# Row pitch of the activation tiles in a two-layer streaming encoder: 320 columns for the matmul inputs, 288, 304, 320 and 256 for the SwiGLU outputs

## The chip, the cores and the metric

The kernel runs on one NeuronCore of a Trainium2 chip. What counts is device time in microseconds (us) of one execution; three runs of a kernel are timed, and their median is taken. The engines are PE (TensorE, matmul; its weight loads are shown apart as PEld), DVE (VectorE), ACT (ScalarE), POOL (GpSimd) and SP, which issues most DMA transfers.

## The reference

The program is a trunk of two layers over 16 meta tokens and 256 frames, 272 tokens of 1024 features, in float32. Layer 0 mixes tokens by differential attention, layer 1 by a sparse attention with an indexer. Each mixer stands between two half-weighted SwiGLU feed-forwards:

```python
for layer in range(DEPTH):                      # DEPTH = 2
    h = h + 0.5 * _swiglu(_rms_norm(h, ln_ffn1[layer]), ffn1_wi[layer], ffn1_wo[layer])
    hn = _rms_norm(h, ln_mix[layer])
    ...
    h = h + mix @ w_out[layer]
    h = h + 0.5 * _swiglu(_rms_norm(h, ln_ffn2[layer]), ffn2_wi[layer], ffn2_wo[layer])
return h[:, N_META:]

def _swiglu(x, wi, wo):                         # wi: 1024 x 5632, wo: 2816 x 1024
    a, b = jnp.split(x @ wi, 2, axis=-1)
    return (jax.nn.silu(a) * b) @ wo
```

## The kernel before

Features lie on the 128 partitions and tokens along the free dimension: `h` is [128, 8, 272], eight rows of 272 tokens in each partition, one row for each block of 128 features. A float32 product is made of three passes in the type float32r, whose values are split into a high and a low part: `mm3` (lines 245 to 248) issues high weights by high rows (L246), high weights by low rows (L247) and low weights by high rows (L248), into one PSUM tile. Each matmul has its own weight load.

`prep_x` scales a row of `h` and splits it into `xh` and `xl`, the tiles that `X["h"]` and `X["l"]` point to. They are the moving operand of the gate-and-up product of every feed-forward and of the projections of both attentions. A feed-forward (`ffn`) first runs over 22 blocks of hidden features: for each it takes one weight tile, and for each of the eight rows k of xh and xl it issues three matmuls into a gate tile `pa` and three into an up tile `pb`, 48 in all. So each row is read by six matmuls in a run. DVE and ACT then form silu(gate) times up and split it into row j of `ah` and `al` (22 rows each). In its second half `ffn` makes eight output blocks from these: for each it runs over the 22 rows of ah and al, three matmuls a row, 66 matmuls into a tile `pc`. There are four feed-forwards. The first three work on 272 tokens; the last one leaves out the meta tokens and works on 256 (`c0=NM`), and its X tiles lie in the storage of the tile `W`, which before held the relative-position bias.

Before the change every one of these rows is 272 columns from the next. The projections of queries and keys in the first attention read the rows of xh and xl in order for one output tile after the other, so each row is read by three matmuls in a run. In the sparse attention, `cqh` and `cql` are the split latent of the queries, [128, 2, 256], the moving operand of `q_abs`.

Weights come from HBM through SP's queue into `wr` tiles; ACT makes the high part `wh`, DVE the low part `wl`, in rotating buffers of 2048 columns. All tiles are placed by pools, in the order in which the code asks for them. In the built program the tiles begin, in bytes within a partition, at 27136 (xh), 35840 (xl), 46720 (W), 152512 and 176448 (ah and al of the first feed-forward), 148224 and 172160 (ah and al of the others), 177536 and 179584 (cqh and cql); the weight buffers begin at 88704 (wh) and 121472 (wl) and every 8192 bytes after these. A matmul reads 128 weight columns, 512 bytes, at a multiple of 512 bytes within its buffer.

Of the kernel before, what the change touches and what calls it, by code (L numbers as in the profile page):

```python
# [11 lines left out]
F32 = mybir.dt.float32  # L12
F32R = mybir.dt.float32r
BF = mybir.dt.bfloat16
AF = mybir.ActivationFunctionType
OP = mybir.AluOpType
# [5 lines left out]
KT = D // 128  # L22
SEQ = 256
NM = 16
T = NM + SEQ
DFF = 2816
FT = DFF // 128
# [5 lines left out]
BH = 16  # L33
IH = 8
NREL = 399

CH = 2048
WARM = 8
# [23 lines left out]
def trunk(ctx, tc, d, out):  # L62
    nc = tc.nc
    PE, ACT, DVE, POOL = nc.tensor, nc.scalar, nc.vector, nc.gpsimd

    const = ctx.enter_context(tc.tile_pool(name="const", bufs=1))
# [6 lines left out]
    ps = ctx.enter_context(tc.tile_pool(name="ps", bufs=1, space=PSUM))  # L73

    def psa():
        return ps.tile([128, 512], F32, name="pa", bufs=3)

    def psb():
        return ps.tile([128, 512], F32, name="pb", bufs=3)
# [90 lines left out]
    h = const.tile([128, KT, T], F32, name="h")  # L170
# [28 lines left out]
    def ln(i):  # L199
        return lambda k: gn[:, 8 * i + k:8 * i + k + 1]  # L200

    X = dict(h=const.tile([128, KT, T], F32R, name="xh"), l=const.tile([128, KT, T], F32R, name="xl"))
    acc = const.tile([128, T], F32, name="acc")
    R = const.tile([128, T], F32, name="R")

# [3 lines left out]

    def prep_x(k, g, c0=0):  # L210
        c = slice(c0, T)
        xh, xl = X["h"], X["l"]
        ACT.activation(xh[:, k, c], h[:, k, c], AF.Copy, scale=g(k))
        DVE.scalar_tensor_tensor(xl[:, k, c], h[:, k, c], g(k), xh.bitcast(F32)[:, k, c],  # L214
                                 op0=OP.mult, op1=OP.subtract)

    def prep_s(k, c0=0):
# [27 lines left out]
    def mm3(ps, wh, wl, bh, bl, start, stop):  # L245
        PE.matmul(ps, wh, bh, start=start, stop=False)  # L246
        PE.matmul(ps, wh, bl, start=False, stop=False)  # L247
        PE.matmul(ps, wl, bh, start=False, stop=stop)  # L248
# [3 lines left out]
    for k in range(KT):  # L252
        c = slice(256 * k, 256 * k + 256)
# [12 lines left out]
    W = const.tile([128, 16, T], F32, name="W")  # L266
# [22 lines left out]
            prep_x(mt, g, c0)  # L289
            prep_s(mt, c0)  # L290

    def ffn(g_next, c0=0, extra=None, first=0):
        c = slice(c0, T)
        with tc.tile_pool(name="act", bufs=1) as actp, tc.tile_pool(name="ev", bufs=2) as ev:
            ah = actp.tile([128, FT, T], F32R, name="ah")
            al = actp.tile([128, FT, T], F32R, name="al")
            ub = {}

            def act_lo(j):
                DVE.tensor_tensor(al[:, j, c], ub.pop(j)[:, c], ah.bitcast(F32)[:, j, c], OP.subtract)  # L300

            def evac(j, pa, pb):
                t = ev.tile([128, T], F32, name="t")
                s = ev.tile([128, T], F32, name="s")
                b = ev.tile([128, T], F32, name="b")
                DVE.tensor_tensor(t[:, c], pa[:, c], R[:, c], OP.mult)  # L306
                last_silu.append(ACT.activation(s[:, c], t[:, c], AF.Silu))
                DVE.tensor_tensor(b[:, c], pb[:, c], R[:, c], OP.mult)
                ws.ahead()
                if j:  # L310
                    act_lo(j - 1)
                DVE.tensor_tensor(b[:, c], s[:, c], b[:, c], OP.mult)  # L312
                ACT.copy(ah[:, j, c], b[:, c])  # L313
                ub[j] = b

            pairs = {}
            for j in range(FT):
                wh, wl = ws.next()
                pa, pb = psa(), psb()
                for k in range(KT):  # L320
                    for m, ps in ((0, pa), (1, pb)):
                        s = slice((2 * k + m) * 128, (2 * k + m + 1) * 128)
                        mm3(ps[:, c], wh[:, s], wl[:, s], X["h"][:, k, c], X["l"][:, k, c],
                            k == 0, k == KT - 1)
                pairs[j] = pa, pb
                if j == first:
                    rstd(psc(), c0)
                    if extra:
                        extra(psc())
                if j >= first:  # L330
                    for i in sorted(pairs):
                        evac(i, *pairs.pop(i))
            act_lo(FT - 1)

            for mt in range(KT):
                ps = psc()
                for half in range(2):
                    wh, wl = ws.next()
                    for kk in range(11):
                        f = half * 11 + kk  # L340
                        s = slice(kk * 128, kk * 128 + 128)
                        mm3(ps[:, c], wh[:, s], wl[:, s], ah[:, f, c], al[:, f, c], f == 0, f == FT - 1)
                    if half == 0:
                        ws.ahead()
                evac_h(mt, ps, True, g_next, c0)
                ws.ahead()

    def diff_attention():
        with tc.tile_pool(name="da", bufs=2) as da, tc.tile_pool(name="dp", bufs=1) as dp:
# [11 lines left out]
            for i in range(2):  # L361
                p = dp.tile([128, 400], F32, name=f"pta{i}")
# [19 lines left out]
            def proj_qk(i):  # L382
                wh, wl = ws.next()
                ps = (psc(), psc()) if i == 1 else (pj(), pj())
                for m in range(2):
                    for k in range(KT):
                        s = slice((2 * k + m) * 128, (2 * k + m + 1) * 128)
                        mm3(ps[m][:, :T], wh[:, s], wl[:, s], X["h"][:, k, :], X["l"][:, k, :], k == 0, k == KT - 1)
                    if i == 0 and m == 0:
                        rstd(ps1())  # L390
                st[i] = dict(ps=ps)
# [21 lines left out]
            def proj_v(i):  # L413
                wh, wl = ws.next()
                ps = pj()
                for k in range(KT):
                    s = slice(k * 128, k * 128 + 128)
                    mm3(ps[:, :T], wh[:, s], wl[:, s], X["h"][:, k, :], X["l"][:, k, :], k == 0, k == KT - 1)
                v = da.tile([128, T], F32, name="v")
                DVE.tensor_tensor(v, ps[:, :T], R, OP.mult)  # L420
                st[i]["v"] = v
# [162 lines left out]
            n = AH  # L584
# [7 lines left out]
            g = [pj(), pj(), None, None]  # L592
# [23 lines left out]
            for grp in (2, 3):  # L616
                w = ws.next()
                for m in range(2):
                    ps = pj()
# [4 lines left out]
    def dsa():  # L624
        q0 = NM
        Q = slice(q0, T)
        with tc.tile_pool(name="sa", bufs=2) as sa, tc.tile_pool(name="sp", bufs=1) as sp, \
# [77 lines left out]
            for m in range(4):  # L705
                ps = ps1()
                for k in range(2):
                    s = slice((2 * m + k) * 128, (2 * m + k + 1) * 128)
# [202 lines left out]
            n = BH  # L911
            for i in range(n):
# [14 lines left out]
                    soft_fin(i - 1)  # L927
                if i >= 3:
                    av(i - 3)
            x2 = const.tile([128, 16, T], F32R, name="W")  # L930
            X["h"], X["l"] = x2[:, 0:KT, :], x2[:, KT:16, :]

            def wout_part(ps, w, m, k0, k1):
                wh, wl = w
# [6 lines left out]
            g = [psc(), None, None, None]  # L941
# [20 lines left out]
            for grp in (2, 3):  # L962
                w = ws.next()
                for m in range(2):
                    ps = psc()
                    wout_part(ps, w, m, 0, 8)
                    evac_h(2 * grp + m, ps, False, ln(5), q0)
                ws.ahead()

    ffn(ln(1), extra=build_bias, first=1)  # L970
    diff_attention()
    once.close()
    ffn(ln(3))
    ffn(ln(4))
    dsa()
    ffn(None, c0=NM)


def _layout(inp):
# [49 lines left out]
    oh = np.zeros((32, 400), f)  # L1029
    for j in range(NREL):  # L1030
        rel = j - 271
# [22 lines left out]
```

## Time and profile before

| | |
|---|---|
| timed runs | 1083.3 us median of 3 (1083.02 to 1084.7) |
| profiled execution | span of 1079.7 us from first to last instruction; no other total of this execution is listed |
| PE | 1067.9 us busy, 8332 matmuls |
| PEld | 1021.7 us busy |
| DVE, ACT, POOL | 689.6, 542.7, 77.2 us busy |
| transfers | 174.20 MB, 161 GB/s on average |

The span is the time between the first and the last instruction of the profiled execution; the timed runs are other executions, and what the runtime adds before and after is in theirs. Matmuls are pipelined: the next one starts long before the record of the last one ends, so start-to-start spacing tells more than a record's length.

### The profile page before, as it was taken

The page shows a single profiled execution, that of the slowest core. Times are in us where ns is not written, and L with a number is a line of the kernel's source. Part 1 is how long each engine was busy: PE and PEld are TensorE (multiplying, and loading weights), DVE is VectorE, ACT ScalarE, POOL GpSimd, SP SyncE. Part 2 cuts the span into 40 slices and gives each one's busy share as a digit, 9 for nine tenths or more (in the row PEclk, how much of TensorE's full clock was granted, in tenths as well). Part 3 has the DMA queues.
Part 4 walks back from the last instruction along what each step waited for, and adds up shares of the span by engine and source line. Part 5 has one row for each costly group of instructions (what it writes and reads, how often), then busy time and mean ns, then how long its engine had stood idle before and what let it go on. Part 6 is the DMA issues. An engine that isn't in the chain of part 4 may idle for free.

```text
span 1079.7 us, 20010 instructions
## 1 busy us (share of the span) xinstructions
PE 1067.9 (99%) x8332; PEld 1021.7 (95%) x8332; DVE 689.6 (64%) x1191; ACT 542.7 (50%) x876; POOL 77.2 (7%) x111
## 2 busy tenths in 40 slices
PE   8999999999999999999999999999999999999998
PEld 7999999998889999999999999999876799999998
DVE  6567645577777666655576666546898657666542
ACT  6455444356687544444454444535856545444331
POOL 1200000042210000000000000000153100000000
PEclk9999999999999999999999999999999999999999
DMA  8985445533343454445654544455422025554461
GB/s 295 210 233 204 151 154 169 190 134 128 128 153 117 166 187 168 172 129 170 213 204 164 188 161 142 161 172 201 156 91 90 1 101 181 189 195 171 147 200 68
DMA packets 30809, 174.20 MB, mean 161 GB/s; under 512 B 3664, under 2 KB 5216, under 8 KB 16896
## 3 DMA queue, kind: packets, MB, share of 16 engines
q1 hardware_dynamic: 29808, 169.99, 46.0%
q0 software_dynamic: 912, 2.95, 1.5%
q8 instruction: 65, 1.06, 0.4%
q14 instruction: 24, 0.20, 0.1%
HBM read 171.47 MB, written 1.46 MB: 160 GB/s over the span
## 4 chain that ended last, share of the span: by engine, by line
PE 92%; DMA 2%; DVE 2%; ACT 1%; issue 1%; POOL 0%; SPq 0%; DVEq 0%; POOLq 0%; ACTq 0%
PE pa L246 11%; PE pa L247 11%; PE pa L248 11%; PE pc L246 9%; PE pc L247 9%; PE pc L248 9%; PE pb L247 8%; PE pb L246 8%; PE pb L248 8%; DMA wr<-w_ffn_wi 2%; PE pc L858 1%; PE pc L861 1%; DVE wl L133 1%; DMA h<-hT 1%; DVE sel L794 1%
## 5 line engine op out<-in xcount | busy, mean ns | idle before, releaser
L116 ACT CAST wh<-wr 128x2048 fp32r<-128x2048 f32 (+3 forms) x180 | 301.0, 1673 | 347.5 <-PE pb L247 176.0
L133 DVE TENSOR_TENSOR wl<-wr,wh 128x2048 fp32r<-128x2048 f32 (+3 forms) x188 | 368.0, 1958 | 48.6 <-PE pc L248 29.4
L246 PE MATMUL pa<-xh,wh 128*128 128x272 f32 (+1 forms) x736 | 213.0, 290 | 2.4 <-ACT wh L255 2.4
L248 PE MATMUL pa<-xh,wl 128*128 128x272 f32 (+1 forms) x736 | 212.7, 289 | 1.5 <-DVE wl L133 1.5
L247 PE MATMUL pa<-xl,wh 128*128 128x272 f32 (+1 forms) x736 | 213.1, 290 | 0.0
L246 PE MATMUL pc<-ah,wh 128*128 128x272 f32 (+1 forms) x704 | 201.6, 286 | 0.0
L247 PE MATMUL pc<-al,wh 128*128 128x272 f32 (+1 forms) x704 | 201.2, 286 | 0.0
L248 PE MATMUL pc<-ah,wl 128*128 128x272 f32 (+1 forms) x704 | 200.9, 285 | 0.0
L247 PE MATMUL pb<-xl,wh 128*128 128x272 f32 (+1 forms) x544 | 157.4, 289 | 0.0
L248 PE MATMUL pb<-xh,wl 128*128 128x272 f32 (+1 forms) x544 | 156.8, 288 | 0.0
L246 PE MATMUL pb<-xh,wh 128*128 128x272 f32 (+1 forms) x544 | 156.0, 287 | 0.0
L246 PEld LDWEIGHTS pa<-xh,wh 128*128 128x128 f32 x736 | 139.0, 189 | 7.3 <-ACT wh L255 3.7
L248 PEld LDWEIGHTS pa<-xh,wl 128*128 128x128 f32 x736 | 138.6, 188 | 2.0 <-DVE wl L133 1.7
L247 PEld LDWEIGHTS pa<-xl,wh 128*128 128x128 f32 x736 | 138.5, 188 | 0.2
L247 PEld LDWEIGHTS pc<-al,wh 128*128 128x128 f32 x704 | 132.6, 188 | 0.0
L248 PEld LDWEIGHTS pc<-ah,wl 128*128 128x128 f32 x704 | 132.5, 188 | 0.0
L246 PEld LDWEIGHTS pc<-ah,wh 128*128 128x128 f32 x704 | 132.3, 188 | 0.0
L306 DVE TENSOR_TENSOR t<-pa,R 128x272 f32<-128x272 f32 (+1 forms) x88 | 38.4, 436 | 117.0 <-PE pa L248 116.6
L246 PEld LDWEIGHTS pb<-xh,wh 128*128 128x128 f32 x544 | 103.1, 189 | 0.0
L247 PEld LDWEIGHTS pb<-xl,wh 128*128 128x128 f32 x544 | 102.5, 188 | 0.2 <-DVE xl L214 0.2
L248 PEld LDWEIGHTS pb<-xh,wl 128*128 128x128 f32 x544 | 102.4, 188 | 0.0
L313 ACT CAST ah<-b 128x272 fp32r<-128x272 f32 (+1 forms) x88 | 36.6, 416 | 75.1 <-DVE b L312 75.1
(326 smaller groups left out, 1723.9 us busy)
## 6 DMA issues: line engine op xcount, KB each, us to landing
wr<-w_ffn_wi SPq DMA_DIRECT2D x85, 1024.0 KB, 4.8
wr<-w_ffn_wo SPq DMA_DIRECT2D x64, 704.0 KB, 4.1
wr<-w_qk SPq DMA_DIRECT2D x8, 1024.0 KB, 4.7
wr<-w_out SPq DMA_DIRECT2D x8, 1024.0 KB, 4.9
wr<-w_v SPq DMA_DIRECT2D x8, 512.0 KB, 3.3
wr<-w_uqa SPq DMA_DIRECT2D x4, 1024.0 KB, 4.8
W<-fd POOLq DMA_DIRECT2D x8, 272.0 KB, 18.9
wr<-w_ffn_wi SPq DMA_DIRECT2D x7, 256.0 KB, 6.5
```

The lines of the kernel that those rows point to most:

```text
L116: ACT.copy(w[:, c], self.raw[i][:, c])
L133: DVE.tensor_tensor(w[:, c], r[:, c], self.h[i].bitcast(F32)[:, c], OP.subtract)
L246: PE.matmul(ps, wh, bh, start=start, stop=False)
L247: PE.matmul(ps, wh, bl, start=False, stop=False)
L248: PE.matmul(ps, wl, bh, start=False, stop=stop)
L306: DVE.tensor_tensor(t[:, c], pa[:, c], R[:, c], OP.mult)
L313: ACT.copy(ah[:, j, c], b[:, c])
L794: DVE.scalar_tensor_tensor(sel[:, b, kc], r[:, kc], wt[:, b, 2 * i + e:2 * i + e + 1], sel[:, b, kc], op0=OP.mult, op1=OP.add)
L858: PE.matmul(ps[:, B1], qas[i][:, 256 * k + 128:256 * k + 256], ckg[:, k, :], start=k == 0, stop=k == 1)
L861: PE.matmul(ps[:, B0], qas[i][:, 256 * k:256 * k + 128], ckg[:, k, 0:144], start=k == 0, stop=k == 1)
```

## The change

Three things change in the layout, and nothing in what is computed. The tiles xh and xl get rows of 320 columns, of which 272 are used (`XS`). The tiles ah and al get rows of 288, 304, 320 and 256 columns in the four feed-forwards (`AS`), and are filled from column 0 also in the last one. The last feed-forward's X tiles are packed to rows of 256 tokens without the meta tokens, with 64 columns left free between the high and the low tile; `X["o"]` is the offset of the first token there. `ffn` is given its number `i`; the loop variable that had this name is now `n`.

The instructions of every engine are the same as before, in the same order. On DVE, after the first attention, two instructions change what they wait for: the first multiplication of the second feed-forward's `t` no longer waits for POOL, and the first `al` does.

Since xh and xl grow by 1536 bytes each, everything behind them moves on by 3072 bytes. In the built program xh begins at 27136 and xl at 37376, W at 49792 (the packed low tile 8448 bytes behind it), ah and al of the four feed-forwards at 155584 and 180928, 151296 and 178048, 151296 and 179456, 151296 and 173824, cqh and cql at 180608 and 182656, wh at 91776 and wl at 124544.

```diff
+XS = 320
+AS = (288, 304, 320, 256)
...
-    X = dict(h=const.tile([128, KT, T], F32R, name="xh"), l=const.tile([128, KT, T], F32R, name="xl"))
+    X = dict(h=const.tile([128, KT, XS], F32R, name="xh"), l=const.tile([128, KT, XS], F32R, name="xl"), o=0)
...
     def prep_x(k, g, c0=0):
         c = slice(c0, T)
-        xh, xl = X["h"], X["l"]
-        ACT.activation(xh[:, k, c], h[:, k, c], AF.Copy, scale=g(k))
-        DVE.scalar_tensor_tensor(xl[:, k, c], h[:, k, c], g(k), xh.bitcast(F32)[:, k, c],
+        xh, xl, xc = X["h"], X["l"], slice(c0 - X["o"], T - X["o"])
+        ACT.activation(xh[:, k, xc], h[:, k, c], AF.Copy, scale=g(k))
+        DVE.scalar_tensor_tensor(xl[:, k, xc], h[:, k, c], g(k), xh.bitcast(F32)[:, k, xc],
...
-    def ffn(g_next, c0=0, extra=None, first=0):
+    def ffn(i, g_next, c0=0, extra=None, first=0):
         c = slice(c0, T)
+        ac = slice(0, T - c0)
+        xc = slice(c0 - X["o"], T - X["o"])
...
-            ah = actp.tile([128, FT, T], F32R, name="ah")
-            al = actp.tile([128, FT, T], F32R, name="al")
+            ah = actp.tile([128, FT, AS[i]], F32R, name="ah")
+            al = actp.tile([128, FT, AS[i]], F32R, name="al")
...
-                        mm3(ps[:, c], wh[:, s], wl[:, s], X["h"][:, k, c], X["l"][:, k, c],
+                        mm3(ps[:, c], wh[:, s], wl[:, s], X["h"][:, k, xc], X["l"][:, k, xc],
...
-                        mm3(ps[:, c], wh[:, s], wl[:, s], ah[:, f, c], al[:, f, c], f == 0, f == FT - 1)
+                        mm3(ps[:, c], wh[:, s], wl[:, s], ah[:, f, ac], al[:, f, ac], f == 0, f == FT - 1)
...
-            x2 = const.tile([128, 16, T], F32R, name="W")
-            X["h"], X["l"] = x2[:, 0:KT, :], x2[:, KT:16, :]
+            x2 = const.tile([128, 17, SEQ], F32R, name="W").rearrange("p k t -> p (k t)")
+            n2 = KT * SEQ
+            X["h"] = x2[:, 0:n2].rearrange("p (k t) -> p k t", t=SEQ)
+            X["l"] = x2[:, n2 + 64:2 * n2 + 64].rearrange("p (k t) -> p k t", t=SEQ)
+            X["o"] = NM
...
-    ffn(ln(1), extra=build_bias, first=1)
+    ffn(0, ln(1), extra=build_bias, first=1)
...
-    ffn(ln(3))
-    ffn(ln(4))
+    ffn(1, ln(3))
+    ffn(2, ln(4))
     dsa()
-    ffn(None, c0=NM)
+    ffn(3, None, c0=NM)
```

## Rows read from the trace of the kernel before

**Rows 1.** The page: busy time, share of the span and instructions; the chain by engine.
```profile
PE 1067.9 (99%) x8332; PEld 1021.7 (95%) x8332; DVE 689.6 (64%) x1191; ACT 542.7 (50%) x876; POOL 77.2 (7%) x111
...
PE 92%; DMA 2%; DVE 2%; ACT 1%; issue 1%; POOL 0%; SPq 0%; DVEq 0%; POOLq 0%; ACTq 0%
```

**Rows 2.** Windows by stage, PE alone: window, its length, busy time, matmuls, clock.
```profile
core 0: us, PE busy (x), PEclk, DMA share, GB/s
145.00:211.00 66.00, 66.00 (x530) 1.00 0.53 176
359.00:480.00 121.00, 121.00 (x970) 1.00 0.48 166
480.90:546.90 66.00, 66.00 (x531) 1.00 0.56 188
679.20:745.00 65.80, 65.80 (x529) 1.00 0.52 175
896.00:1013.80 117.80, 117.80 (x1009) 1.00 0.51 181
1014.00:1076.00 62.00, 62.00 (x528) 1.00 0.43 144
```

**Rows 3.** One line, the full-precision logits of the sparse attention: min/median/max ns.
```profile
L858 PE MATMUL pc<-ckg,qa x48: 392/393/497, 816.8 to 858.6; 128*128 128x272 f32 x48
```

**Rows 4.** Groups by form, PE, second feed-forward's gate-and-up product (359 to 480 us).
```profile
L247 PE MATMUL pb<-xl,wh 128*128 128x272 f32 x162 | 46.8, 289 | 0.0
L248 PE MATMUL pa<-xh,wl 128*128 128x272 f32 x162 | 46.7, 288 | 0.0
L247 PE MATMUL pa<-xl,wh 128*128 128x272 f32 x161 | 46.7, 290 | 0.0
L248 PE MATMUL pb<-xh,wl 128*128 128x272 f32 x162 | 46.6, 288 | 0.0
L246 PE MATMUL pb<-xh,wh 128*128 128x272 f32 x162 | 46.4, 286 | 0.0
L246 PE MATMUL pa<-xh,wh 128*128 128x272 f32 x161 | 45.8, 284 | 0.0
```

**Rows 5.** The same view for one run of row 0, 372.96 to 373.45 us.
```profile
L247 PE MATMUL pb<-xl,wh 128*128 128x272 f32 x1 | 0.3, 292 | 0.0
L248 PE MATMUL pa<-xh,wl 128*128 128x272 f32 x1 | 0.3, 290 | 0.0
L246 PE MATMUL pa<-xh,wh 128*128 128x272 f32 x1 | 0.3, 288 | 0.0
L247 PE MATMUL pa<-xl,wh 128*128 128x272 f32 x1 | 0.3, 288 | 0.0
L248 PE MATMUL pb<-xh,wl 128*128 128x272 f32 x1 | 0.3, 288 | 0.0
L246 PE MATMUL pb<-xh,wh 128*128 128x272 f32 x1 | 0.3, 285 | 0.0
```

**Rows 6.** One tile, cqh, 770 to 802 us: min/median/max ns.
```profile
L246 PE MATMUL pb<-cqh,wh x58: 278/283/388, 769.7 to 801.2; 128*128 128x256 f32 x58
L248 PEld LDWEIGHTS pb<-cqh,wl x58: 187/192/192, 769.9 to 801.4; 128*128 128x128 f32 x58
L248 PE MATMUL pb<-cqh,wl x58: 278/283/283, 770.0 to 801.5; 128*128 128x256 f32 x58
```

**Rows 7.** One tile, W, 896 to 1013.8 us: the last feed-forward's gate-and-up product.
```profile
L247 PE MATMUL pa<-W,wh x168: 274/280/283, 896.1 to 1013.3; 128*128 128x256 f32 x168
...
L246 PEld LDWEIGHTS pb<-W,wh x168: 187/188/188, 896.2 to 1013.4; 128*128 128x128 f32 x168
L246 PE MATMUL pb<-W,wh x168: 276/279/282, 896.3 to 1013.5; 128*128 128x256 f32 x168
```

**Rows 8.** Timeline, PE, sparse attention's query projection; 29 matmuls between the two.
```profile
791.03 0.28 PE L247 MATMUL pb<-cql,wh 128*128 128x256 f32 x1
...
794.63 0.28 PE L247 MATMUL pb<-cql,wh 128*128 128x256 f32 x1
```

**Rows 9.** Timeline, PE, first attention's projection; 47 matmuls between the two.
```profile
217.59 0.29 PE L246 MATMUL pa<-xh,wh 128*128 128x272 f32 x1
...
223.65 0.29 PE L246 MATMUL pc<-xh,wh 128*128 128x272 f32 x1
```

More of the change, by code (lines that the diff above doesn't have):

```diff
@@ L290, in evac_h @@
             prep_s(mt, c0)
-    def ffn(g_next, c0=0, extra=None, first=0):
+    def ffn(i, g_next, c0=0, extra=None, first=0):
         c = slice(c0, T)
+        ac = slice(0, T - c0)
+        xc = slice(c0 - X["o"], T - X["o"])
         with tc.tile_pool(name="act", bufs=1) as actp, tc.tile_pool(name="ev", bufs=2) as ev:
-            ah = actp.tile([128, FT, T], F32R, name="ah")
-            al = actp.tile([128, FT, T], F32R, name="al")
+            ah = actp.tile([128, FT, AS[i]], F32R, name="ah")
+            al = actp.tile([128, FT, AS[i]], F32R, name="al")
             ub = {}
             def act_lo(j):
-                DVE.tensor_tensor(al[:, j, c], ub.pop(j)[:, c], ah.bitcast(F32)[:, j, c], OP.subtract)
+                DVE.tensor_tensor(al[:, j, ac], ub.pop(j)[:, c], ah.bitcast(F32)[:, j, ac], OP.subtract)
             def evac(j, pa, pb):
@@ L312, in evac @@
                 DVE.tensor_tensor(b[:, c], s[:, c], b[:, c], OP.mult)
-                ACT.copy(ah[:, j, c], b[:, c])
+                ACT.copy(ah[:, j, ac], b[:, c])
                 ub[j] = b
@@ L330, in ffn @@
                 if j >= first:
-                    for i in sorted(pairs):
-                        evac(i, *pairs.pop(i))
+                    for n in sorted(pairs):
+                        evac(n, *pairs.pop(n))
             act_lo(FT - 1)
@@ L387, in proj_qk @@
                         s = slice((2 * k + m) * 128, (2 * k + m + 1) * 128)
-                        mm3(ps[m][:, :T], wh[:, s], wl[:, s], X["h"][:, k, :], X["l"][:, k, :], k == 0, k == KT - 1)
+                        mm3(ps[m][:, :T], wh[:, s], wl[:, s], X["h"][:, k, 0:T], X["l"][:, k, 0:T], k == 0, k == KT - 1)
                     if i == 0 and m == 0:
@@ L417, in proj_v @@
                     s = slice(k * 128, k * 128 + 128)
-                    mm3(ps[:, :T], wh[:, s], wl[:, s], X["h"][:, k, :], X["l"][:, k, :], k == 0, k == KT - 1)
+                    mm3(ps[:, :T], wh[:, s], wl[:, s], X["h"][:, k, 0:T], X["l"][:, k, 0:T], k == 0, k == KT - 1)
                 v = da.tile([128, T], F32, name="v")
```

## The prediction

> **What bounds the kernel now.** I read the page first. PE is busy for 99% of the span, and 92% of the chain that ended last is PE work [rows 1]; the granted clock is 1.00 in every stage that I looked at [rows 2], which is the upper of its two levels (2.4 GHz). The spacing of the matmuls therefore sets the time, so the second view was busy time by stage. In stages without a gap, the length of the window divided by its matmuls is the spacing from one start to the next. A window counts the matmuls that its edges cut as well: a record lasts 0.29 us while the next one starts after 0.12 us, so two are to be taken off [rows 2]. That gives:
>
> - gate-and-up product of the second feed-forward, 272 columns: 121.00 us / 968 = 125.0 ns
> - down products of the first, second and third feed-forward, 272 columns: 66.00 / 528 = 125.0, 66.00 / 529 = 124.8, 65.80 / 527 = 124.9 ns
> - gate-and-up product of the last one, 256 columns: 117.80 / 1007 = 117.0 ns
> - its down product, 256 columns: 62.00 / 526 = 117.9 ns
>
> At 2.4 GHz, 272 columns take 113.3 ns and 256 columns 106.7 ns if one column enters in each cycle. Some 10% is lost, and this loss is what a row's place in memory could change. That the chip can do without it shows in the full-precision matmuls of the attention: a record lasts 393 ns for 272 columns in two passes [rows 3]. A record is longer than the spacing by about 162.5 ns, since its end is modelled: in the gate-and-up product the six places have means from 284 to 290 ns, 287.5 on average [rows 4], where the spacing is 125.0. So 393 ns stands for 230.5 ns, or 115 ns a pass, and this I take as the spacing without a stall.
>
> **What the change does.** No instruction is added or removed and none is moved on any engine; two waits on POOL change places on DVE after the first attention, long after POOL's last work there, which costs nothing. ACT and DVE write as many columns as before, each row in one piece, and no DMA changes. What is left is where rows start. A row of 272 columns is 1088 bytes, four times 256 plus 64, so from one row of the contraction to the next the start moves on by 64 bytes in 256, and four starts take turns. 320 columns are five times 256 bytes: every row of xh and xl now starts at a multiple of 256. All weight buffers lie 128 past a multiple of 256, before and after.
>
> **Does the start matter at all?** In the second feed-forward, the six matmuls of row 0, whose start is a multiple of 256, last 288, 288, 290, 285, 292 and 288 ns [rows 5], 288.5 on average against 287.5 for the stage: 126.0 instead of 125.0 ns. So the start that the change gives to all rows belongs to the slower ones, by 1 ns.
>
> **A stage whose rows all have one start.** The projection of the queries in the sparse attention reads cqh and cql: 256 columns, a pitch of 256, every row 128 past a multiple of 256. Its records have a median of 283 ns and reach no more than 283 in the row for the low weights [rows 6]; those of the last feed-forward's gate-and-up product, as wide but with four starts in turn, have medians of 279 and 280 [rows 7]. Start to start it is 30 matmuls in 794.63 - 791.03 = 3.60 us, 120.0 ns without change [rows 8]: a beat into which the matmuls settle, 3.0 ns slower than with four starts. The weight loads under it also take longer, a median of 192 against 188 ns [rows 6, 7]. Weight load and moving rows seem to get into each other's way, at the same place each time.
>
> **The sum, term by term** (number of matmuls by change of spacing):
>
> 1. Gate-and-up products 1 to 3: 3 x 22 x 48 = 3168 matmuls, 125.0 now. The nearest row for what comes is row 0, 126.0; the far one is the settled beat, which adds 3.0: 128.0. I take 126.5, nearer to row 0, which has the same width and start: +1.5 ns, +4.8 us.
> 2. Projections of both attentions that read xh and xl with 272 columns: 576 + 72 = 648. Here each row is read by three matmuls in a run, not six; 48 spacings take 223.65 - 217.59 = 6.06 us, 126.2 ns [rows 9]. To 126.5: +0.2 us.
> 3. Down product of the third feed-forward, pitch 320, every row of ah and al on a multiple of 256: 528 x (126.5 - 124.9) = +0.8 us.
> 4. Down product of the first, pitch 288, two starts in turn (192 and 64 past a multiple): neither is the slow one of row 0, nor is it one start; 0, with 528 x 1 ns = 0.5 us to either side. Down product of the second, pitch 304: the same four starts in the opposite order; 0.
> 5. Gate-and-up product of the last one: 22 x 48 = 1056 matmuls, 256 columns, pitch 256, all rows 128 past a multiple. This is cqh and cql again, in width, pitch, start and order of the weights: 117.0 to 120.0, +3.2 us.
> 6. Its down product, pitch 256, all rows on a multiple of 256: 528 matmuls at 117.9 now, between that and 120.0 then; I take 119.0, +0.6 us.
>
> Sum: 4.8 + 0.2 + 0.8 + 3.2 + 0.6 = +9.6 us on a span of 1079.7, so 1089.3. Between this span and the median of the timed runs, 1083.3, lie 3.6 us, in which nothing changes: 1092.9, about 1093 us, or 0.9% slower. This case's own range has row 0 alone in terms 1 and 3 (126.0: +3.2 +0.6, and term 2 at -0.1), 3.2 for term 5 and 0 for term 6: +6.9, 1090; at the other end 128.0 in terms 1 to 3 (+9.5 +1.2 +1.6) and 120.0 in the last two (+3.2 +1.1): +16.6, 1100.
>
> PE's neighbours stay covered: in the gate-and-up product the page's DVE and ACT work lies below a PE that never pauses, and a slower PE only gives them more room.
>
> **A rule that speaks against it.** Rows show a loss of 10% against one column a cycle [rows 2], and weight loads of 192 ns where moving rows have one start [rows 6]. The Trainium skill says otherwise: its page "SBUF — State Buffer", section "Who interferes with whom", holds that PE never waits for anyone at SBUF, and "TensorE: Matmul & The Clock Gate", section "Step-by-step: what each phase is for", that rows and weights are read through two independent ports, so that a load takes no bandwidth from a running matmul. By these the start of a row would be worth nothing, each term above 0 and the time 1083.3; the trace does not bear it out, since 125.0 ns stands where its own formula, in "Back-to-back issue gap", would give an estimate of 115.8.
>
> **The rivals.**
>
> - *No change.* If the spacing is set by something that merely comes round every four rows, such as the order of the weights, the starts do not matter: terms all 0, 1083 us. Row 0's 1 ns could be this. Against it: the settled 120.0 and the 192 ns loads, in a stage whose weights come in the same order as those of the last feed-forward. It also comes out so if a gain in one stage pays for a loss in another. Chance 0.12.
> - *Faster.* With one start for all rows the matmuls settle into one beat, and which beat depends on the distance between the rows' start and the weights' start. In cqh it is 0 bytes in 256; for xh and xl it is 128 instead, so weight load and moving rows may fall between one another and not on one another. The fastest of the six places now has 284 ns, 121.5 ns of spacing [rows 4]. If all rows of terms 1 to 3 come to that: 3168 x 3.5 + 648 x 4.7 + 528 x 3.4 = 15.9 us; half of it is 8 us; with term 5 unchanged or won as well, 1064 to 1075. The extreme is no stall at all, 115 ns: 4344 matmuls by 10 ns, 43 us, 1040, for which only full-precision passes speak. It decides from the point where term 1 falls below 125.0 - 4800 / 3168 = 123.5 ns, for then the other terms (+4.8 us) are made up. For it: no stage of the trace has 272 columns with one start, so its beat is unknown. Against it: row 0 has the same distance and is slow. Chance 0.30.
> - *Much slower.* The settled beat of xh and xl lies above 128.0: over 1101 us. Single places last up to 292 ns in row 0, that is 129.5. Chance 0.08.
>
> **Chances and range.** The forecast has 0.50, the others 0.12, 0.30 and 0.08. A measurement of this kernel tells a change from none at about 0.2%, 2 us. Slower: 0.50 + 0.08 = 0.58, faster 0.30, the same 0.12. For the range I go up to 1101, which leaves out the much slower 0.08, and down to 1068, which leaves out the better third of the faster case, some 0.10.
>
> **What would show it.** In the changed kernel's profile the spacing by stage is the test. Right: about 126.5 ns in the gate-and-up products 1 to 3, with the six places no longer changing from row to row, 120.0 in the last one with weight loads of 192 ns, and 125 in the down product with pitch 304. Wrong in its mechanism: the last gate-and-up product stays at 117.0, or the four-row pattern lives on with one start. Wrong in sign: the gate-and-up products fall below 123.5. Three feed-forwards with three pitches also tell how much each is worth by itself.

## The result and the profile after

The changed kernel takes 1095.4 us (median of 4 runs, 1090.6 to 1096.5) where the kernel before took 1083.8 beside it (4 runs, 1083.0 to 1084.7): a ratio of the means of 1.0098, 95% interval 1.0072 to 1.0124. The medians are 11.6 us apart and the means 10.6 us, with an interval of 7.8 to 13.4 us. That is about 1% slower; the forecast was 1093. The profiled execution has a span of 1093.3 us (its own time 1095.1), at a mean granted clock of 0.998.

Two lines of the page of the changed kernel: busy time, and the chain that ended last by engine.

```profile
PE 1080.7 (99%) x8332; PEld 1034.5 (95%) x8332; DVE 689.8 (63%) x1191; ACT 542.8 (50%) x876; POOL 77.1 (7%) x111
...
PE 91%; DMA 3%; DVE 2%; ACT 1%; issue 1%; POOL 0%; SPq 0%; DVEq 0%; ACTq 0%; POOLq 0%
```

Against [rows 1] the counts are equal, DVE, ACT and POOL are as busy as before, and only PE (+12.8 us) and its weight loads (+12.8 us) have grown. So the same matmuls come at a longer spacing. The windows by stage of the changed kernel, PE alone, answer to [rows 2]. The columns are window, length, busy time, matmuls, clock, DMA share, GB/s.

```profile
150.20:216.00 65.80, 65.80 (x528) 1.00 0.53 175
400.00:440.00 40.00, 40.00 (x318) 1.00 0.53 182
488.20:554.00 65.80, 65.80 (x527) 1.00 0.56 187
600.00:640.00 40.00, 40.00 (x318) 1.00 0.49 178
688.60:755.00 66.40, 66.40 (x526) 1.00 0.53 173
905.00:1027.00 122.00, 122.00 (x1018) 1.00 0.50 177
1027.20:1089.00 61.80, 61.80 (x523) 1.00 0.43 144
```

Length divided by (matmuls - 2) is the spacing, to 0.1 or 0.2 ns. The lines are the first down product, the second gate-and-up product (40.00 / 316 = 126.6 ns), the second down product (65.80 / 525 = 125.3), the third gate-and-up and the third down product (66.40 / 524 = 126.7), and the last gate-and-up (122.00 / 1016 = 120.1) and last down product (61.80 / 521 = 118.6). From here on a spacing is the mean from start to start of neighbouring matmuls of a stage, from the trace's start times with pauses left out. It agrees with such windows and does not suffer from the few records that a trace lacks:

| stage (matmuls) | before, ns | after, ns | worth, us |
|---|---|---|---|
| gate-and-up 1, 2, 3 (3 x 1056) | 125.02 each | 126.65, 126.66, 126.66 | +5.2 |
| projections, 272 columns (648) | 126.04 | 126.63 | +0.4 |
| down 1, 2 (528 each) | 125.21, 124.94 | 125.18, 125.36 | +0.2 |
| down 3 (528) | 124.94 | 126.67 | +0.9 |
| gate-and-up of the last (1056) | 116.96 | 120.00 | +3.2 |
| down of the last (528) | 117.93 | 118.67 | +0.4 |

The sum is +10.3 us, each line being matmuls times difference. Groups by form, PE, 360 to 487 us of the changed kernel, where all rows of xh and xl have one start (compare [rows 4]); lines 248 to 250 are now the three passes:

```profile
L248 PE MATMUL pa<-xh,wh 128*128 128x272 f32 x167 | 49.0, 293 | 0.0
L250 PE MATMUL pa<-xh,wl 128*128 128x272 f32 x167 | 48.8, 292 | 0.0
L249 PE MATMUL pb<-xl,wh 128*128 128x272 f32 x166 | 48.5, 292 | 0.0
L250 PE MATMUL pb<-xh,wl 128*128 128x272 f32 x167 | 48.0, 288 | 0.0
L249 PE MATMUL pa<-xl,wh 128*128 128x272 f32 x167 | 48.0, 288 | 0.0
L248 PE MATMUL pb<-xh,wh 128*128 128x272 f32 x167 | 48.0, 288 | 0.0
```

The beat is now short and repeats: three of the six places last 288 ns and three 292 or 293, where six places lay between 284 and 290 before. The mean went from 287.5 to 290.2, more than the spacing did (1.6 ns), since the ends are modelled; the beat is to be read here, not the price. And tile W in the last gate-and-up product, 905 to 1027 us, min/median/max in ns:

```profile
L249 PE MATMUL pb<-W,wh x170: 280/283/283, 904.8 to 1026.9; 128*128 128x256 f32 x170
...
L248 PEld LDWEIGHTS pa<-W,wh x169: 188/192/192, 904.9 to 1026.3; 128*128 128x128 f32 x169
```

This is what cqh and cql showed [rows 6]: 283 ns, and weight loads of 192 ns instead of the 188 of [rows 7].

The span of the profiled execution grew by 13.6 us, 3.3 more than the spacings give. These lie in the first gate-and-up product. Windows of two of its tiles in the changed kernel, all engines:

```profile
core 0: us, PE busy (x) PEld busy (x) DVE busy (x) ACT busy (x) POOL busy (x), PEclk, DMA share, GB/s
54.10:60.80 6.70, 6.49 (x51) 6.17 (x49) 2.03 (x5) 2.66 (x3) 0.00 (x0) 1.00 1.01 206
60.80:70.60 9.80, 7.83 (x49) 7.61 (x49) 5.63 (x7) 4.79 (x5) 0.00 (x0) 0.83 0.70 230
```

A tile of 48 matmuls takes 6.08 us here; the second of these took 9.8. PE stands idle for 9.80 - 7.83 = 1.97 us, and the granted clock of the stretch is 0.83. The timeline of PE there gives start, length, and in brackets the idle time ahead and what ended it:

```profile
63.23 0.40 PE L250 MATMUL pa<-xh,wl 128*128 128x272 f32 x1 [1.97 <-DVE wl L135]
63.46 0.29 PE L248 MATMUL pb<-xh,wh 128*128 128x272 f32 x1
...
64.66 0.43 PE L248 MATMUL pa<-xh,wh 128*128 128x272 f32 x1
64.89 0.43 PE L249 MATMUL pa<-xl,wh 128*128 128x272 f32 x1
```

The low weights come late. PE goes on at the upper level, and from 64.66 us to 67.8 a record is 0.43 us long and the next start comes after 0.23 us, twice the 113.3 ns of 272 columns at 2.4 GHz: the lower level, 1.2 GHz. The kernel before has such a pause one tile later, 1.47 us in front of its line 248 at 67.02 us, and no slow matmuls behind it. Experiments 10 and 11 return to this.

### The profile page after: what moved, and what is told of

Read it like the earlier page. It is cut to its first block, busy times and chain, and to the rows that moved or that the text cites. A ratio compares the mean times of both kernels' runs of the same rounds, so it can differ in the third digit from the quotient of the medians.

```text
span 1093.3 us, 20010 instructions
## 1 busy us (share of the span) xinstructions
PE 1080.7 (99%) x8332; PEld 1034.5 (95%) x8332; DVE 689.8 (63%) x1191; ACT 542.8 (50%) x876; POOL 77.1 (7%) x111
## 4 chain that ended last, share of the span: by engine, by line
PE 91%; DMA 3%; DVE 2%; ACT 1%; issue 1%; POOL 0%; SPq 0%; DVEq 0%; ACTq 0%; POOLq 0%
PE pa L248 11%; PE pa L250 10%; PE pa L249 10%; PE pc L248 9%; PE pc L249 9%; PE pc L250 9%; PE pb L249 8%; PE pb L248 8%; PE pb L250 8%; DMA wr<-w_ffn_wi 3%; PE pc L862 1%; DVE wl L135 1%; PE pc L865 1%; DVE sel L798 1%; ACT wh L118 1%
## 5 line engine op out<-in xcount | busy, mean ns | idle before, releaser
L248 PE MATMUL pa<-xh,wh 128*128 128x272 f32 (+1 forms) x736 | 217.4, 296 | 2.4 <-ACT wh L257 2.4
L250 PE MATMUL pa<-xh,wl 128*128 128x272 f32 (+1 forms) x736 | 214.9, 292 | 2.3 <-DVE wl L135 2.2
```

## Experiments

A row's start is given in bytes past a multiple of 256, and its **distance** is the row's start minus the weights' start, modulo 256. The weights start at 128 unless said otherwise. Theory: the spacing is a function of that distance. Rivals: it is a function of the row's own start, or of the order in which starts come round. In the kernels below `XS` and `AS` are the pitches; `XO` holds column offsets of the rows of xh and xl, one pair for each stage in order (first feed-forward, first attention, second and third feed-forward, sparse attention), `X3` the same for the last feed-forward, and `AO` those of ah and al in the four feed-forwards; 16 columns are 64 bytes. Experiments 3, 4, 6, 7 and 8 were executed once each, so their total times are not compared; what is read from them is the spacing by stage, at a granted clock of 1.00. The edits are against the changed kernel unless said otherwise; `...` marks lines left out, in experiments 1 to 8 the code that takes up these constants.

**1 and 2. The two halves of the change alone.** The first keeps only the pitch of xh and xl, with the last X tiles as before the change; the second undoes that pitch and keeps everything else.

```diff
 XS = 320
-AS = (288, 304, 320, 256)
+AS = (T, T, T, T)
...
```
```diff
-XS = 320
+XS = T
 AS = (288, 304, 320, 256)
...
```

> Only xh and xl get rows of 320 columns; ah, al and the last feed-forward's input keep the layout of before. If the cost is spacing and adds up by stage: 126.65 ns in the gate-and-up products 1 to 3 and in the projections, everything else as before, so 3 x 1.7 + 0.4 = +5.6 us, a ratio of about 1.005. If the 3 us of waiting for weights that the changed kernel's first feed-forward shows belong to the input pitch as well, +8.5 us, 1.008, with the wait at 54 to 77 us. If stages influence one another, neither.

> xh and xl back at 272 columns; the pitches of ah and al and the packed input of the last feed-forward as changed. If the cost adds up by stage: 125.0 ns in the gate-and-up products 1 to 3; 126.67 in the third down product, 120.0 in the last gate-and-up product, 118.7 in the last down product: 0.2 + 0.9 + 3.2 + 0.4 = +4.7 us, a ratio of about 1.0043. If the wait of the first feed-forward comes with these tiles, +7.7 us, 1.007.

Measured, beside 1084.67 for the kernel before: 1088.35 us, ratio 1.0036 (1.0022 to 1.0051), and 1088.67 us, 1.0038 (1.0022 to 1.0055). In the first the gate-and-up products go to 126.66 and the projections to 126.6, and everything else stays; in the second the gate-and-up products stay at 125.02, and the third down product (126.66), the last gate-and-up (119.99) and the last down product (118.67) move as in the whole change. The expected 1.005 lies at the upper edge of the first interval, the expected 1.0043 inside the second. So each stage answers to its own rows alone; by time the halves add up to 1.0074, which lies inside the interval of the whole.

**3. Other starts, each in a stage of its own.**

```diff
-AS = (288, 304, 320, 256)
+AS = (320, 320, 320, 256)
+XO = ((16, 16), (0, 32), (32, 32), (48, 48), (0, 0))
+AO = ((32, 32), (0, 32), (16, 48), (0, 0))
+X3 = (32, 96)
...
```

> Constant starts again, but other ones. Rows of xh and xl start 64 (first feed-forward), 128 (second) and 192 (third) past a multiple of 256, in the first attention 0 for xh and 128 for xl; ah and al have a pitch of 320 and start at 64 and 64, 0 and 128, 64 and 192; the last input starts at 0 with 0 in the last ah and al. Theory of one start: with every constant start the matmuls settle, one value per stage, but the value depends on the start: 128 is where the weights start and should be the slowest, near 128 ns; 64 and 192 should lie below 126.6, perhaps below the 125.0 of four starts in turn. Rival, that any constant start costs the same: 126.65 in all three gate-and-up products and 126.67 in the down products. Both expect 118.7 in the last gate-and-up product, since start 0 gave that in the last down product, and not 120.0.

Windows by stage of this kernel, PE alone:

```profile
146.60:211.40 64.80, 64.80 (x527) 1.00 0.54 177
360.00:420.00 60.00, 60.00 (x481) 1.00 0.49 171
...
600.00:640.00 40.00, 40.00 (x318) 1.00 0.54 185
```

In order: first down product, start 64 (64.80 / 525 = 123.4 ns); second gate-and-up, start 128 (60.00 / 479 = 125.3); third gate-and-up, start 192 (40.00 / 316 = 126.6). The first gate-and-up product, start 64 as well, has 123.36. So start 64 is faster than any stage of 272 columns in the kernel before, two stages with other tiles and the same start agree to 0.03 ns, and the start counts. That 128 would be the slow one was wrong: it is 125.34; and 192, expected below 126.6, is no faster than start 0 was. Where high and low rows have two different starts, the second and third down products have 124.43 and 124.47 ns. In the first attention (xh at 0, xl at 128) some groups of 48 matmuls have 126.6 and others about 124.5, although the layout is the same for all of them; experiment 4 comes back to this.

**4. The weights moved, not the rows.** A tile of 128 bytes ahead of the weight buffers puts the weights on a multiple of 256. xh, xl and W stay where they are; ah, al, cqh and cql lie behind the weights and move with them.

```diff
+    shift = ctx.enter_context(tc.tile_pool(name="shift", bufs=1))
+    shift.tile([128, 32], F32, name="shift")
...
```

> The changed kernel with a tile of 128 bytes put before the weight buffers: xh, xl and the last input stay where they are, weights and all that lies behind them (ah, al, cqh, cql) move by 128 bytes. Theory of distance: only the distance between row start and weight start counts. The down products (126.7 third, 118.7 last) and the query projection (120.0) keep their spacing, since both sides moved; the last gate-and-up product comes to distance 128, so from 120.0 to 118.7; the gate-and-up products 1 to 3 come to distance 0, from 126.65 to about 128. Rival, that the row's own start counts and the weights do not: gate-and-up products unchanged at 126.65 and 120.0, while the last down product goes from 118.7 to 120.0 and the query projection from 120.0 to 118.7.

Windows of the second gate-and-up, the second down and the last gate-and-up product, then tile W in the last:

```profile
420.00:480.00 60.00, 60.00 (x481) 1.00 0.46 154
485.40:551.00 65.60, 65.60 (x526) 1.00 0.56 187
...
900.00:1020.00 120.00, 120.00 (x1012) 1.00 0.50 176
```

```profile
L260 PEld LDWEIGHTS pa<-W,wh x169: 187/188/189, 899.9 to 1019.9; 128*128 128x128 f32 x169
```

The second and third gate-and-up products, whose rows did not move, go from 126.66 to 125.34, what experiment 3 had at distance 0 with other addresses. The last one goes from 120.00 to 118.67 and its weight loads from 192 back to 188 ns; 118.67 is also what experiment 3 had there at the same distance of 128. The down products, whose rows moved by 128 bytes together with the weights, keep 125.19, 125.33, 126.64 and 118.67, and so does the query projection (119.5 before the move, 119.7 after it, short waits between its groups included). So the row's own start as the cause falls, and the place of the rows against the weights counts. The size that was expected for distance 0 did not come.

That the spacing is a function of the distance alone does not hold, however. The first gate-and-up product of this run has the same distance of 0, and its first tiles keep 126.67 ns. At 54.34 us one matmul starts late, 0.22 us after the one ahead of it instead of 0.13 us, and from there on the spacing is 125.3 ns. Windows on either side of that place:

```profile
29.68:53.98 24.30, 24.30 (x194) 1.00 1.02 202
82.80:149.00 66.20, 66.20 (x530) 1.00 0.49 170
```

That is 24.30 / 192 = 126.6 and 66.20 / 528 = 125.4 ns. The first attention shows it too: four groups of 48 matmuls have 126.67 ns, most others 125.2 to 125.6. So one layout can hold two beats. What makes the matmuls take one or the other is not shown.

**5. Start 64 for all rows of 272 columns,** with the last feed-forward laid out as before.

```diff
-AS = (288, 304, 320, 256)
+AS = (320, 320, 320, T)
+XO = ((16, 16),) * 5
+AO = ((32, 32), (16, 16), (16, 16), (NM, NM))
...
```

> Every row of xh, xl, ah and al with 272 columns starts 64 past a multiple of 256, that is 192 (mod 256) from the weights; pitch 320 throughout; the last feed-forward keeps the layout of before. Theory of distance: what the first feed-forward of e3_other_starts showed at this start, 123.36 and 123.33 ns, holds at every place: gate-and-up products 125.02 to 123.36 (3168 x 1.66 = 5.3 us), projections 126.1 to 123.4 (648 x 2.7 = 1.7 us), down products 1 to 3 from 125.2 and 124.9 to 123.33 (528 x 5.1 = 2.7 us): 9.7 us faster than before, a ratio of 0.991. Rival, that 123.36 belonged to the first feed-forward and not to the start: the other stages do not follow, and the gain is at most 1.8 + 1.0 = 2.8 us, 0.9974.

Measured: 1073.42 us (1072.5 to 1075.4) beside 1084.28, ratio 0.9900 (0.9886 to 0.9914). The windows are those of the second gate-and-up and the second down product:

```profile
360.00:420.00 60.00, 60.00 (x489) 1.00 0.51 176
...
478.40:543.00 64.60, 64.60 (x526) 1.00 0.57 191
```

60.00 / 487 and 64.60 / 524 are both 123.3 ns (123.34 and 123.33 from start to start), the projections have 123.47, the last two products stay at 116.96 and 117.93. Against before, with the first attention's 576 projections, that is 3168 x 1.68 + 576 x 2.57 + 528 x (1.88 + 1.61 + 1.61) ns = 5.3 + 1.5 + 2.7 = 9.5 of the 10.9 us. A pitch of 320 columns costs 0.4% in xh and xl at start 0; at start 64, in ah and al too, it gains 1.0%.

**6. Finer starts:** 32, 96 and 80 for xh and xl, 48, 16 and 112 for ah and al, and in the last feed-forward 64 and 192.

```diff
+XO = ((8, 8), (16, 16), (24, 24), (20, 20), (0, 0))
+AS = (320, 320, 320, 320)
+AO = ((28, 28), (4, 4), (28, 28), (48, 48))
+X3 = (48, 112)
...
```

> Starts between the steps of 64, pitch 320: rows of xh and xl at 32, 96 and 80 in the three gate-and-up products, ah and al at 48, 16 and 112; 64 in the first attention; last input at 64 and last ah and al at 192, 256 columns each. If the memory is read in units of 64 bytes, a start within a unit counts as that unit's start or costs one unit more: 32, 48 and 16 like 0 (126.66) or worse, 96, 80 and 112 like 64 (123.36) or worse. If only the distance in bytes counts, values between the neighbours, some perhaps below 123.3. At 256 columns the starts 64 and 192 are new: between 116 and 120 ns.

Windows of the first gate-and-up product (start 32), the first down product (48) and the third gate-and-up product (80):

```profile
90.00:145.00 55.00, 55.00 (x448) 1.00 0.45 154
148.50:213.00 64.50, 64.50 (x525) 1.00 0.53 177
...
560.00:620.00 60.00, 60.00 (x476) 1.00 0.47 166
```

They have 55.00 / 446 = 123.3, 64.50 / 523 = 123.3 and 60.00 / 474 = 126.6 ns. With units of 64 bytes, starts 32 and 48 would have cost as much as start 0 or more, so that theory falls; but 80 does not lie between its neighbours 64 and 128 either. With experiments 3 to 5 this gives, for 272 columns with one start in high and low rows:

| distance | 0 | 64 | 128 | 144 | 160 | 176 | 192 | 208 | 224 | 240 |
|---|---|---|---|---|---|---|---|---|---|---|
| ns | 125.34 | 126.66 | 126.66 | 124.44 | 123.33 | 123.34 | 123.34 | 126.66 | 125.39 | 125.00 |

The values are means of a whole stage; at distance 0 the other beat of 126.67 ns is left out, and the distances 144, 160, 176, 208, 224 and 240 rest on one stage each. There is a plateau from 160 to 192 with a steep edge behind it: 16 bytes on cost 3.3 ns. For 256 columns it is 120.00 at distance 0, 117.78 at 64 and at 192, 118.67 at 128, and four starts in turn (116.96) beat them all.

**7. High and low rows at different starts.** xh at 64 with xl at 0, 128 and 192; ah and al at 0 and 64, 192 and 64, 128 and 64.

```diff
+XO = ((16, 0), (16, 16), (16, 32), (16, 48), (0, 0))
+AS = (320, 320, 320, 320)
+AO = ((16, 32), (48, 16), (32, 16), (0, 16))
+X3 = (48, 128)
...
```

> High and low rows at different starts, pitch 320: xh at 64 with xl at 0, 128 and 192 in the three gate-and-up products; ah at 0, 192 and 128 with al at 64; 256 columns: xh 128 past with xl at 64, ah at 0 with al at 64. If each matmul has the spacing of its own start (64: 123.36, 0 and 192: 126.66, 128: 125.34), a third of the matmuls weighs as much: 124.5, 124.0, 124.5 in the gate-and-up products and 125.6, 125.6, 124.7 in the down products. If what one matmul leaves behind counts for the next, other values, and the fit by single starts falls.

Windows of the first down product (ah 0, al 64), the second gate-and-up (xh 64, xl 128) and the second down product (ah 192, al 64):

```profile
148.90:215.30 66.40, 66.40 (x526) 1.00 0.53 173
360.00:420.00 60.00, 60.00 (x484) 1.00 0.50 176
...
483.80:549.00 65.20, 65.20 (x527) 1.00 0.56 188
```

They have 126.65, 124.45 and 124.48 ns, and the other two gate-and-up products 124.5 and 124.45. If each matmul cost what its own distance costs in the table, ah 0 with al 64 would have (2 x 126.66 + 123.34) / 3 = 125.6, and ah 192 with al 64 the same; they have 126.65 and 124.48. In the same way xh 64 with xl 0 or 192 would have 124.45, which is what came, but xl 128 would have 124.0 and has 124.45. That each matmul costs what its own distance says, whatever stands beside it, falls.

**8. The low weights alone moved by 64 bytes.** A tile of 64 bytes between the two pools puts wl at 192 and leaves wh at 128. High rows at 64 and low rows at 128 in the first two feed-forwards, both at 64 in the third.

```diff
+    shift = ctx.enter_context(tc.tile_pool(name="shift", bufs=1))
+    shift.tile([128, 16], F32, name="shift")
...
+XO = ((16, 32), (16, 32), (16, 32), (16, 16), (0, 0))
+AS = (320, 320, 320, T)
+AO = ((16, 32), (0, 16), (0, 0), (NM, NM))
...
```

> The low weights alone move by 64 bytes (192 past a multiple of 256, the high ones stay at 128). In the first two feed-forwards high rows start at 64 and low rows at 128, in the third all rows start at 64; the last one is laid out as before. Theory A, the weights that are loaded while a matmul runs (those of the next one) count: then every load of the first two feed-forwards lies 192 from the rows that run over it, and gate-and-up and down products take about 123.3 ns there, as with start 64 for all; the third takes 124.4. Theory B, the matmul's own weights count: in the first two the second pass lies at distance 0 and the third at 128, so about 125 ns; the third 124.4. Theory C, the spacing follows the rows' starts alone, whatever the weights do: 124.45 in the first two, as high 64 with low 128 had before, and 123.3 in the third.

Windows of the second and the third down product:

```profile
484.60:550.40 65.80, 65.80 (x526) 1.00 0.56 187
...
685.00:751.40 66.40, 66.40 (x527) 1.00 0.52 172
```

65.80 / 524 = 125.6 ns in the second down product (125.55 from start to start, as in the second gate-and-up and the first down product) and 66.40 / 525 = 126.5 (126.66, as in the third gate-and-up product) in the third. Theory A wanted 123.3 and 124.4, theory B 125 and 124.4, theory C 124.45 and 123.3. B alone is near in the first two; none is right in the third, where one pass of three at distance 128 costs as much as all three do. So wl's place counts as well as wh's, and how the three passes combine stays open.

The first gate-and-up product again holds two beats in one layout. Its windows ahead of a pause of 0.56 us at 54.28 us, and later:

```profile
29.84:53.31 23.47, 23.47 (x194) 1.00 1.01 210
75.72:147.70 71.98, 71.98 (x576) 1.00 0.53 180
```

That is 23.47 / 192 = 122.2 ns, below every value of the table above, and 71.98 / 574 = 125.4 ns (125.6 from start to start). The change comes with the pause and not with the transfers: right behind it, from 54.6 to 60.0 us, the spacing is 125.6 ns while the DMA share is still 1.05.

**9. Start 64, and the last down product with high and low rows at one start,** four starts taking turns (pitch 336). The diff is against experiment 5.

```diff
-AS = (320, 320, 320, T)
-AO = ((32, 32), (16, 16), (16, 16), (NM, NM))
+AS = (320, 320, 320, 336)
+AO = ((32, 32), (16, 16), (16, 16), (NM, NM + 32))
```

> All rows of 272 columns start at 64, and the rows of the last down product get a pitch of 336 columns, so that high and low rows of the same number start at the same place and four starts take turns. By the distance theory the 272-column stages stay at 123.3 ns, the last gate-and-up product stays at 117.0, and the last down product falls from 117.9 to 117.0: 0.5 us less than the kernel with start 64 alone, a ratio of about 0.9895 to the kernel before. If the order of the two tiles counts and not their starts, 117.9 stays and the ratio is 0.990.

Missed: the last down product went up to 118.35 ns, 1074.86 us in all, ratio 0.9912 (0.9895 to 0.9928). Its rows change start after three matmuls, those of the last gate-and-up product after six; whether that keeps 116.96 from carrying over was not tried. Experiment 5 keeps the lowest median of the complete kernels, though the two intervals overlap.

**10 and 11. The pause in the first feed-forward.** On GpSimd's queue nine transfers of the relative-position bias run while it happens. Both kernels set the bias to zero instead, so that part of the computation is left out.

```diff
-        fd = dram.tile([16, 16, 400], F32, name="fd")
-        nc.gpsimd.dma_start(fd, f[:, None, :].to_broadcast([16, 16, 400]))
-        for a in range(8):
-            ...
-            nc.gpsimd.dma_start(W[16 * a:16 * a + 16], src)
+        POOL.memset(W, 0.0)
```

> The kernel before without the nine transfers of the relative-position bias on GpSimd's queue; the bias is set to zero instead, so that part of the computation is left out. Theory: the waits for weights in the first feed-forward come from these transfers. Then the first gate-and-up product loses the waits between tiles 6 and 10, a few us, and the kernel is about 3 us faster than the kernel before (1080 to 1081); the spacing stays at 125.0. Rival: the waits come from the weight stream alone and stay.

> The changed kernel with the same part left out. If the spacing sums and the rest of the difference is those waits, it is 10.2 us slower than the kernel before with the same part left out, about 1090 to 1091. If the waits have another cause that the change makes worse, the distance stays at 11.6 us or more.

Measured beside 1084.19: the kernel before without the loads 1080.43 us (1079.5 to 1081.4), ratio 0.9964 (0.9952 to 0.9977); the changed one without them 1090.43 us (1089.6 to 1091.0), 1.0057 (1.0039 to 1.0076). For 5 to 150 us PE's view of waits has one line left, all of it before 15 us; here that of the changed one:

```profile
PE pa L248 <- ACT wh L257: 2.7, 3, 1.8
```

and windows of three tiles at the same place show PE without a gap at a granted clock of 1.00:

```profile
53.70:59.80 6.10, 6.10 (x51) 6.10 (x50) 3.83 (x6) 2.66 (x3) 0.00 (x0) 1.00 0.49 180
59.80:65.80 6.00, 6.00 (x49) 6.00 (x49) 3.74 (x6) 2.66 (x3) 0.00 (x0) 1.00 0.49 161
65.80:71.90 6.10, 6.10 (x50) 6.10 (x49) 3.84 (x6) 2.66 (x3) 0.00 (x0) 1.00 0.48 173
```

The DMA share in them is 0.5 where it was 1.01 and 0.70. So the bias loads make the weights late, in both kernels. Without them the two kernels are 10.0 us apart, where the spacings alone say 10.3. The scatter shrinks too: 1.9 us over ten runs instead of 7.2 us over the 16 of the kernel before.

## Why the prediction was right

- **What bounds the kernel.** Right: instructions, other engines and transfers did not change, and the spacing gives 10.3 us, where the medians are 11.6 and the means 10.6 us apart. In the profiled pair 3.3 us more lie in pauses of the first feed-forward, and experiments 10 and 11 show the bias loads as their source; the sum held nothing for them. That they make the timed difference larger is not shown: 10.0 us without the loads lies within the interval of 7.8 to 13.4 us. Nor is it shown why the changed kernel pauses for longer in its profiled run.
- **Terms 1 to 3.** 126.5 was forecast for every stage with rows on a multiple of 256; measured are 126.66 (gate-and-up), 126.63 (projections) and 126.67 (third down product). The choice nearer to row 0's 126.0 than to 128.0 was right: +6.5 us against +5.8. The lower bound was well founded, since row 0 had the distance of 128 that all rows now have. The upper one was not: the 3.0 ns that one start costs 256 columns at distance 0 do not carry over. There 272 columns settle at 125.34 ns, 0.3 above the mixture of before, or at 126.67 (experiment 4). That a value chosen between these two came within 0.2 ns was in part luck.
- **Term 4.** 0 for pitches 288 and 304: -0.03 and +0.42 ns, -0.02 and +0.2 us. That four starts in the opposite order make no difference is not quite so.
- **Term 5.** The analogy with cqh and cql held to the last digit: 120.00 ns, loads of 192 ns, +3.2 us.
- **Term 6.** 119.0 was forecast, 118.67 came: +0.4 instead of +0.6 us. The sum was 0.7 us too small in all.
- **The rival of no change** fell: every stage whose rows all went to one start changed its spacing, and so did the gate-and-up products when nothing but the weights moved against their rows. The Trainium skill's rule of "TensorE: Matmul & The Clock Gate", section "Step-by-step: what each phase is for", that rows and weights come through two independent ports, so that a load takes no bandwidth from a running matmul, would leave no such effect; this kernel's times do not bear it out. When the weights moved by 128 bytes against rows that stayed, 126.66 ns became 125.34, and 120.00 ns became 118.67 with loads of 188 ns instead of 192 (experiment 4). The 115.8 ns that the prediction held against the rule is weaker evidence: the Trainium skill's section "Back-to-back issue gap" gives that formula for an isolated matmul, and says of a stream of load and matmul pairs that both set the spacing.
- **The faster rival** had the right mechanism, the place of the rows against the weights, and the wrong distance. The 128 that the change gives to xh and xl has the slowest beat of the table, together with 64 and 208; 160 to 192 go below its point of decision, 123.5 ns, and experiment 5 shows what that is worth. The trace of before could have told more than row 0 did. From 360 to 480 us its rows at distance 0, 64, 128 and 192 have 125.4, 125.1, 125.8 and 123.7 ns (240 matmuls each): the class at 128, into which the change puts all rows, is the slowest, and the class at 192 the fastest. Of the other two the mixture gives the wrong order: with one start, 64 has 126.66 and 0 has 125.34 ns.

## What to carry to other kernels

Where PE never pauses and each matmul of 256 or 272 columns loads its own weights, look at where the moving rows start against the weights, modulo 256 bytes, before a pitch is chosen: the worst place and the best here were 3.3 ns of 125 apart, 2.7% of the stage. A pitch by itself decides nothing; 320 columns lose at one start and win at another. Take the classes of rows that a trace already holds, compare their spacing, and test one start per stage in a single kernel, since each stage answers for itself. Then look along each stage tile by tile: one layout can hold two beats, and a pause can move it from one to the other (experiments 4 and 8).

## What the runs showed of the hardware

- Spacing depends on the distance of row start and weight start in 256 bytes, from 123.33 to 126.66 ns for 272 columns with one start, and from 116.96 to 121.07 for 256 (the last with ah at 0 and al at 64, experiment 7), at a granted clock of 1.00. In the second gate-and-up product of the changed kernel, rows at even and at odd multiples of 256 have 126.66 and 126.67 ns, so no period of 512 shows.
- The distance alone does not fix it: 126.67 and 125.34 ns both occur at distance 0 (experiment 4), and 122.2 and 125.6 ns in one product of experiment 8. The change from one to the other came at a late start or a pause; in the other kernels the first gate-and-up product kept its beat through its pauses.
- Most settled beats come in steps: three matmuls take 366.6 (experiment 8), 370.0, 373.3, 376.6 or 380.0 ns, some 3.3 ns apart, which is 8 cycles at 2.4 GHz; 125.34 and 125.00 do not fit quite.
- Low and high weights at different distances count together, and one of three passes at distance 128 can cost as much as all three (126.66 ns, experiment 8). By what rule is open; no run settled it.
- A pause of 1.97 us in PE's stream was followed, 1.4 us after its end, by 3.2 us at 1.2 GHz (64.7 to 67.8 us of the changed kernel); these 14 spacings of 227 instead of 127 ns lose 1.4 us more, so the pause cost 1.7 times its length. After 1.47 us in the kernel before, the clock stayed at 1.00, but so it did after pauses of 1.96, 1.96 and 1.97 us at the same place in experiments 2, 8 and 9: the length of the pause alone does not decide.
